# Seams of an eleven-tile feed-forward: spreading a norm's stores, a third early row tile, blocks between products

## Chip, cores and metric

The kernel runs on one core of one Trainium2 chip. The metric is device microseconds (us) of one execution; lower is better. TensorE (PE) has a granted clock of two levels, 1.2 and 2.4 GHz; the profile writes 1.00 where all of a stretch ran at 2.4 GHz.

## The reference, cut to what matters

One layer over 1024 tokens of width 1024, all in float32: a mixing stage (two recurrences), cross-attention into 256 memory tokens, a SwiGLU feed-forward of width 2816, and a final norm.

```python
h = h + (gate_a * y_a + gate_b * y_b) @ w_out
u = rmsnorm(h, norm_xa_g); m = rmsnorm(mem, norm_mem_g)
q = u @ xa_wq; k = m @ xa_wk; v = m @ xa_wv        # 4 heads of 256
h = h + softmax(q k^T / 16) v @ xa_wo
u = rmsnorm(h, norm_ffn_g)
h = h + (silu(u @ ffn_w1) * (u @ ffn_w3)) @ ffn_w2
return rmsnorm(h, norm_final_g)
```

## The kernel before

**Numbers.** Every float32 operand is split in two parts, `hi` (a copy rounded to the matmul's type) and `lo` (source minus hi); a product is three matmuls, hi·hi, hi·lo and lo·hi (`mm3`, L298). `split` (L278) writes hi on ScalarE (ACT) at L281 and lo on GpSimd (POOL) or VectorE (DVE) at L285.

**Order of work.** The mixing stage (about 0 to 1300 us) has its order written out by hand. All that follows is ordered by the framework when the kernel is compiled: each engine gets one queue, filled by priority (position in the program; a block of `high_priority` moves its instructions ahead) among what the framework's own estimate holds ready. On the chip each queue then runs strictly in that order, and an instruction whose operand is late holds all behind it. Nearly all DMAs are issued on SyncE's queue (SP), so a store that waits for its data holds the loads behind it.

**Attention** (`attention_block`, about 1300 to 1710 us). At its start the first block of `xa_wv` is loaded on ACT's queue and split, both at high priority (L1681), while the last steps of mixing (`sa`, its store to `y_d`, and two key products `pproj<-mT,wkey`) are still to run. K and V follow, block by block, then the output projection of mixing (`w_out`, tiles `pw`), the heads, and the output projection of attention (`xa_wo`, `pw` again), which runs once for each half of 512 tokens. Each projection has 4 column blocks; `load_w` loads and splits four weight tiles for each. Beside the projections `w2_sums` (L1707) makes four sums of blocks of `ffn_w2` for each of 11 rows f: load `y` (2 DMAs of 512 KB), two DVE and two POOL subtractions (L1717 to L1720), and a store of 1 MB to `wsum_d`. Seven rows go beside `w_out` and four beside the first half's `xa_wo`. `add_project` stores the new residual `h_d` after all of a half is done.

**Feed-forward, first part** (about 1710 to 2170 us). The two halves of tokens, of hidden rows and of model columns form 2x2 blocks, multiplied with 7 products in place of 8 (P1 to P7). P5 and P4 need only blocks of the second half of tokens (`S1`, `B22`), which exist before attention is through. For the first AHEAD = 2 of 11 row tiles they are made early (`early_products`, L2035), with weights loaded at high priority, and kept in SBUF (tag `kept`, 14 buffers). Then `late_blocks` (L1947) loads the first operands' rows back (`hn`), normalizes them, and in four steps k transposes them (tiles `pth`) and makes the five other blocks (B11, B21, S3, S2, S4). Then `products(f)` runs for 11 row tiles; it loads the same weights again (tag `wraw`, 10 buffers).

**Feed-forward, second part** (about 2175 to 2380 us). Seven blocks b of 11 items f each. An item is a load of an activation tile `tl` (hidden rows or their sums), a load of a weight tile `wraw`, ACT's `th` and `wh`, DVE's `tl` minus `th` (L2201), POOL's `wl` (through `operand`, L1927), and four `mm3`, which are 12 matmuls of 128x512. Loads run 8 items ahead and splits 4. When a block is done, its function (`p1`, `p6`, `p5`, `p7` or `add`) adds the four sums to the residual `hres`. A list `later` postpones some of these adds, one for each following item. When block 4 is done the first half is complete, and `add` calls `finish` for its four row tiles at once: two DVE scalings (L2139, L2143) and two stores to the output. Block 6 does this for the second half, at the very end.

Of the kernel before, what the change touches and what calls it, by code (L numbers as in the profile page):

```python
# [183 lines left out]
def tile_trunk(ctx, tc, x, mem, norm_mix_g, w_in, rw_mu, rw_w0, rw_w2, rw_a0, rw_a2, rw_g2,  # L184
# [1462 lines left out]
    def attention_block(xctx):  # L1647
# [11 lines left out]
        px = xctx.enter_context(tpool(name="xa_x", bufs=3, space=PSUM))  # L1659
        W = 256  # L1660

        def load_w(src, col, lo_eng=None, queue=nc.sync):

            s3 = src[0, :, col:col + W].rearrange("(k p) c -> p k c", p=P)
            w = []
            for k in range(0, KT, 2):
                raw = rp.tile([P, 2, W], F32, tag="wraw", name="wraw")
                queue.dma_start(out=raw, in_=s3[:, k:k + 2, :])
                hi, lo = (wp.tile([P, 2, W], F32R, tag=n, name=n) for n in ("whi", "wlo"))
# [8 lines left out]
        Vl = vp.tile([P, NMT, D], F32R, tag="Vl", name="Vl")  # L1678
        mT = [act1.tile([P, 2, 4, NM], F32R, tag=n, name="mT") for n in ("ah", "al")]
        with tc.high_priority(4000):  # L1680
            w0 = load_w(xa_wv, 0, queue=nc.scalar)  # L1681
            for n in range(2):
                for e in range(2):
                    nc.sync.dma_start(out=mT[e][:, n].bitcast(F32).rearrange("p k t -> p (k t)"), in_=md[e, n])
        for c in range(D // W):
            if 2 * c >= KEYS:
                w = load_w(xa_wk, c * W)
                for t in range(2):
                    ps = pp.tile([P, HALF], F32, tag="proj", name="pk")
                    for k in range(KT):  # L1690
                        mm3(ps[:, 0:NM], w[k][0][:, t * P:(t + 1) * P], w[k][1][:, t * P:(t + 1) * P],
                            *(m[:, k // 4, k % 4, :] for m in mT), k == 0, k == KT - 1)
                    h = Kh[:, 2 * c + t, :]
                    nc.scalar.activation(h, ps[:, 0:NM], AF.Copy)
                    nc.vector.tensor_tensor(Kl[:, 2 * c + t, :], ps[:, 0:NM], h.bitcast(F32), op=ALU.subtract)
            w = load_w(xa_wv, c * W) if c else w0
            ps = pp.tile([P, NMT, W], F32, tag="proj", name="pvv")
            for t in range(NMT):
                for k in range(KT):
                    mm3(ps[:, t, :], *(m[:, k // 4, k % 4, t * P:(t + 1) * P] for m in mT), *w[k], k == 0, k == KT - 1)  # L1700
            h = Vh[:, :, c * W:(c + 1) * W]
# [5 lines left out]
        def w2_sums(fs, places):  # L1707


            def load(f, y):  # L1710
                for r in range(2):
                    rows = slice((f + r * HF) * P, (f + r * HF + 1) * P)
                    nc.sync.dma_start(out=y[:, 2 * r:2 * r + 2, :].rearrange("p c t -> p (c t)"), in_=ffn_w2[0, rows, :])

            def sums(f, y):
                y11, y12, y21, y22 = (y[:, n, :] for n in range(4))
                nc.vector.tensor_tensor(y11, y12, y11, op=ALU.subtract)  # L1717
                nc.gpsimd.tensor_tensor(y12, y22, y12, op=ALU.subtract)
                nc.gpsimd.tensor_tensor(y22, y22, y11, op=ALU.subtract)
                nc.vector.tensor_tensor(y21, y22, y21, op=ALU.subtract)  # L1720
                nc.sync.dma_start(out=wsd[f], in_=y)

            loaded = []
            for place in places:
                if place:
                    y = place()
                    f = next(fs)
                    load(f, y)
                    loaded.append((f, y))
                    if len(loaded) < 3:  # L1730
                        yield
                        continue
                if loaded:
                    sums(*loaded.pop(0))
                yield
            for l in loaded:
                sums(*l)
                yield

        def add_project(a, w, src, halves, ss=None, beside=iter(()), every=False):  # L1740


            hs = []
            for c in range(D // W):
                ww = load_w(w, c * W)
                for i2 in range(2 * halves.start, 2 * halves.stop):
# [9 lines left out]
                    for n in range(2):  # L1756
                        o = hs[2 * i2 + n - 4 * halves.start][:, c * W:(c + 1) * W]
                        nc.vector.tensor_tensor(o, ps[:, n, :], o, op=ALU.add)  # L1758
                        if ss is not None:
                            junk = sp.tile([P, D], mybir.dt.bfloat16, tag="junk", name="junkw", bufs=1)[:, 0:W]  # L1760
                            nc.scalar.activation(junk, o, AF.Square, accum_out=ss[:, 2 * i2 + n - 4 * halves.start, c:c + 1])
                    if every or c > 1 or c == 1 and i2 % 2:
                        next(beside, None)
            return hs
# [35 lines left out]
        def in_act2(tag, n):  # L1800
# [3 lines left out]
                return pairs[tag][:, n]  # L1804
            return place

        hs = add_project(yT, w_out, x[0], range(NHALF), every=True, beside=w2_sums(
            w2f, [None, None] + [in_act2(tag, n) for tag in ("ah", "al", "ah") for n in range(2)] + [in_act2("al", 0)]))
        xaT = []
        for h in range(NHALF):  # L1810
            for i in range(4):
# [75 lines left out]
                prev = attended(oT[h], hd, next(wt))  # L1887
        for _ in prev:
            pass
        in_kv = [lambda p=p, t=t: p.tile([P, 4, HALF], F32, tag=t, name="y2")  # L1890
                 for p, t in ((kp, "Kh"), (kp, "Kl"), (vp, "Vh"), (vp, "Vl"))]

        for h in range(NHALF):
            hs = add_project(oT, xa_wo, h1d, range(h, h + 1), *((ssq, early_blocks(hs, *fa)) if h else ()),
                             **({} if h else dict(beside=w2_sums(w2f, in_kv), every=True)))
# [31 lines left out]
    def operand(t, name):  # L1927
        if isinstance(t, tuple):
            return t
        hi, lo = (wp.tile(list(t.shape), F32R, tag=n, name=n + name, bufs=7) for n in ("wh", "wl"))  # L1930
        split(hi, lo, t)
        return hi, lo

    def psum(name):
# [11 lines left out]
    def late_blocks():  # L1946
# [22 lines left out]
        for k in range(HK):  # L1969
# [47 lines left out]

    tt = nc.vector.tensor_tensor

    def weights(f):  # L2020

        return [[raw(w, k, (f + e) * P, HK, P) for e in (0, HF) for k in (0, HK)] for w in WS]

    def early_operands(A):
        T1, T4 = [], []
# [9 lines left out]
    def early_products(f, T1, T4):  # L2035

        for name, T, b in (("P5", T1, "S1"), ("P4", T4, "B22")):
            for n in range(2):
                t = kept[f, name, n] = fp.tile([P, HALF], F32, tag="kept", name=name, bufs=14)
                nc.scalar.activation(t, product(name, T[n], B[b]), AF.Copy)  # L2040

    def products(f, A):
        U2, U3, P7, T1 = [], [], [], []
# [47 lines left out]
    next(late)  # L2091
    for f in range(AHEAD):
# [23 lines left out]
    def add(h, i, c, acc, op, first):  # L2116
# [17 lines left out]
    def finish(h, i, c, order):  # L2134
        r = ss[h][:, 3, i:i + 1]
        rows = slice((4 * h + i) * P, (4 * h + i + 1) * P)
        o1, o2 = hs[h][:, 2 * i + 1 - c, :], hs[h][:, 2 * i + c, :]
        if h == 0:
# [3 lines left out]
        nc.sync.dma_start(out=out[rows, (1 - c) * HALF:(2 - c) * HALF], in_=o1)  # L2142
        ins = nc.vector.scalar_tensor_tensor(o2, o2, r, fgs[c], op0=ALU.mult, op1=ALU.mult).ins  # L2143
        if order:
            behind(ins, order)
        nc.sync.dma_start(out=out[rows, c * HALF:(c + 1) * HALF], in_=o2)

    def more(h, i, c, t):
        o = hs[h][:, 2 * i + c, :]
        tt(o, o, t, op=ALU.add)  # L2150

    later = []

    def p1(i, acc):
        nc.scalar.activation(U[i], acc, AF.Copy)
        later.append((0, i, 0, U[i]))

    def p6(i, acc):
        tt(U[i], acc, U[i], op=ALU.add)

    def p5(i, acc):
        tt(V[i], acc, U[i], op=ALU.add)
        later.append((0, i, 1, V[i]))
        later.append((1, i, 1, V[i]))

    def p7(i, acc):
        tt(U[i], acc, U[i], op=ALU.add)
        later.append((1, i, 0, U[i]))
        add(1, i, 1, acc, ALU.add, True)

    w2 = lambda r, c: lambda f: raw(ffn_w2, f + r * HF, c * HALF, 1, HALF)
# [25 lines left out]
    def split_item(b, f):  # L2197
# [10 lines left out]
    for n, (b, f) in enumerate(items):  # L2208
# [47 lines left out]
```

## Time and profile before

| what | value |
|---|---|
| median of 3 runs | 2383.24 us (2382.25 to 2384.34) |
| profiled execution | 2381.83 us |
| its span, first to last instruction | 2380.1 us |
| PE busy | 2311.5 us, 97% of the span |
| PE idle | 68.6 us |
| mean granted clock of PE | 0.990 |
| DVE, ACT, POOL busy | 64%, 48%, 52% |

A group of rows below names its view. A row of the timeline gives start, duration, engine, line, operation, out<-in, count, and in brackets the idle time of the engine before it with what ended that. A row of the windows gives a stretch, its length, busy time and count of PE, weight loads, DVE, ACT and POOL, the granted clock of PE, the busy share of the DMA engines and their rate.

### The profile page before, as it was taken

How to read it: one execution, taken by the hardware profiler on the slowest of the kernel's cores; microseconds unless marked ns; L12 is line 12 of the kernel's file. 1: busy time of each engine (PE TensorE's matmuls, PEld its weight loads, DVE VectorE, ACT ScalarE, POOL GpSimd, SP SyncE). 2: the span in 40 equal slices, each digit the busy share in tenths (PEclk: the TensorE clock that was granted, in tenths of full speed). 3: DMA queues.
4: the chain of work that ended last, by engine and by line, in shares of the span. 5: the costliest groups of instructions: out<-in, count | busy, mean ns of one | idle time of the engine just before them, and what ended most of it. 6: DMA issues, size and time to landing. Idle time of an engine off the chain costs nothing. (4 is left out here: it accounts for less than half of the span.)

```text
span 2380.1 us, 48890 instructions
## 1 busy us (share of the span) xinstructions
PE 2311.5 (97%) x19126; PEld 1913.0 (80%) x19126; DVE 1515.4 (64%) x2397; ACT 1136.1 (48%) x2271; POOL 1235.6 (52%) x1257
## 2 busy tenths in 40 slices
PE   7999999999999999999999999999989999999997
PEld 5777777778887878888887998889968888888876
DVE  5887874667777667766755545444577565566454
ACT  6545454545566646565564515442452333334432
POOL 3554545555566555675564741113465655556544
PEclk9999999999999999999999999999999999999999
DMA  5444445333334344434244893128643433348552
GB/s 176 116 126 119 124 119 166 70 95 85 103 102 121 78 130 107 114 90 115 64 150 142 272 339 128 63 70 305 201 136 100 128 100 100 111 151 319 181 173 93
DMA packets 397668, 325.97 MB, mean 137 GB/s; under 512 B 107467, under 2 KB 330813, under 8 KB 396029
## 3 DMA queue, kind: packets, MB, share of 16 engines
q1 hardware_dynamic: 395005, 317.08, 43.9%
q0 software_dynamic: 1344, 4.72, 0.5%
q8 instruction: 151, 2.47, 0.4%
q10 hardware_dynamic: 1088, 1.05, 0.1%
q14 instruction: 80, 0.66, 0.1%
HBM read 226.03 MB, written 96.21 MB: 135 GB/s over the span
## 5 line engine op out<-in xcount | busy, mean ns | idle before, releaser
L102 PE MATMUL pproj<-uh,whi 128*128 128x512 f32 x768 | 320.3, 417 | 0.9 <-DVE q L102 0.7
L102 PE MATMUL pproj<-uh,wlo 128*128 128x512 f32 x768 | 301.0, 392 | 3.2 <-POOL wlo L102 2.3
L102 PE MATMUL pproj<-ul,whi 128*128 128x512 f32 x768 | 301.4, 392 | 0.0
L285 POOL TENSOR_TENSOR wl<-wraw,wh 128x512 fp32r<-128x512 f32 x143 | 202.0, 1427 | 153.3 <-ACT wh L281 139.9
L285 POOL TENSOR_TENSOR wlo<-wraw,whi 128x512 fp32r<-128x512 f32 (+1 forms) x86 | 118.3, 1380 | 227.7 <-ACT whi L281 219.1
L281 ACT ACTIVATE whi<-wraw 128x512 fp32r<-128x512 f32 (+1 forms) x166 | 101.0, 617 | 188.4 <-DMA wraw<-in_w_out_dram 46.1
L102 POOL TENSOR_TENSOR wlo<-wraw,whi 128x512 fp32r<-128x512 f32 x96 | 128.5, 1349 | 119.3 <-ACT whi L102 106.2
L299 PE MATMUL pproj<-uh,whi 128*128 128x512 f32 (+1 forms) x432 | 179.7, 416 | 0.9 <-ACT whi L281 0.6
L301 PE MATMUL pproj<-uh,wlo 128*128 128x512 f32 (+1 forms) x432 | 170.9, 396 | 1.2 <-POOL wlo L285 1.2
L102 PEld LDWEIGHTS pproj<-uh,whi 128*128 128x128 f32 x768 | 144.4, 188 | 34.1 <-DVE q L102 2.0
L300 PE MATMUL pproj<-ul,whi 128*128 128x512 f32 (+1 forms) x432 | 170.7, 395 | 0.0
L102 PEld LDWEIGHTS pproj<-ul,whi 128*128 128x128 f32 x768 | 144.4, 188 | 32.4
L102 PEld LDWEIGHTS pproj<-uh,wlo 128*128 128x128 f32 x768 | 145.0, 189 | 28.8 <-POOL wlo L102 2.7
L300 PE MATMUL pw<-wlo,ah 128*128 128x256 f32 x512 | 146.7, 287 | 6.9 <-POOL wlo L285 4.6
L299 PE MATMUL pw<-whi,ah 128*128 128x256 f32 x512 | 146.1, 286 | 1.3 <-DVE tok L1758 1.3
L301 PE MATMUL pw<-whi,al 128*128 128x256 f32 x512 | 145.8, 285 | 0.0
L285 POOL TENSOR_TENSOR wlT<-wraw,whT 128x512 fp32r<-128x512 f32 x70 | 98.5, 1419 | 68.9 <-ACT whT L281 49.4
L299 PE MATMUL acc<-wh,th 128*128 128x512 f32 x308 | 121.5, 395 | 7.2 <-ACT wh L281 7.2
L2201 DVE TENSOR_TENSOR tl<-tl,th 128x512 fp32r<-128x512 f32 x77 | 77.1, 1028 | 79.1 <-ACT th L2200 75.2
L281 ACT ACTIVATE wh<-wraw 128x512 fp32r<-128x512 f32 x143 | 86.4, 622 | 82.5 <-PE P L300 57.3
L300 PE MATMUL acc<-wl,th 128*128 128x512 f32 x308 | 122.2, 397 | 2.0 <-POOL wl L285 2.0
L102 ACT ACT_TABLE_LOAD x90 | 115.5, 1283 | 13.5 <-DVE m L102 6.4
(456 smaller groups left out, 6551.9 us busy)
## 6 DMA issues: line engine op xcount, KB each, us to landing
wraw<-in_w_in_dram SPq DMA_DIRECT2D x148, 256.0 KB
wraw<-in_ffn_w_dram SPq DMA_DIRECT2D x137, 256.0 KB
y<-in_ffn_w_dram SPq DMA_DIRECT2D x22, 512.0 KB
wsum_d<-y SPq DMA_DIRECT2D x11, 1024.0 KB
hsum_d<-s SPq DMA_DIRECT2D x44, 256.0 KB
tl<-hsum_d SPq DMA_DIRECT2D x44, 256.0 KB
wraw<-wsum_d SPq DMA_DIRECT2D x44, 256.0 KB
hid_d<-s SPq DMA_DIRECT2D x33, 256.0 KB
```

The lines of the kernel that those rows point to most:

```text
L102: r = getattr(self.engine, op)(*a, **kw)
L281: nc.scalar.activation(hi, src, AF.Copy)
L285: e.tensor_tensor(lo, src, hi.bitcast(F32), op=ALU.subtract)
L299: nc.tensor.matmul(ps, ah, bh, start=first, stop=False)
L300: nc.tensor.matmul(ps, ah, bl, start=False, stop=False)
L301: nc.tensor.matmul(ps, al, bh, start=False, stop=last)
L2201: tt(hl, hl.bitcast(F32), hh.bitcast(F32), op=ALU.subtract)
```

## The change

It changes six places. (1) Only the first `xa_wv` loads keep the high priority; their splits go to their place in the program. (2) `w2_sums` gets a list of steps, one for each group of `w_out` (8 rows: loads in groups 2, 4, 8 and 11, sums in groups 4, 5, 6, 8, 10, 12, 13 and 14) and of the first half's `xa_wo` (3 rows, in V's buffers alone). (3) The stores of `h_d` go into `add_project`. (4) AHEAD is 3; the first two tiles load in the order that T1 needs, the third at its place after the fifth early product; `late_blocks` gives one step k after the 6th, 8th, 10th and 12th early product. (5) In the second part `lo` of the weights goes to DVE for 8 of 11 items and to POOL for 3. (6) For the first half `finish` puts two scalings and a pair of stores for each row tile on `later`, and `later` gives two entries for an item while it is longer than 11.

```diff
@@ attention_block @@
         with tc.high_priority(4000):
-            w0 = load_w(xa_wv, 0, queue=nc.scalar)
+            w0 = list(load_raw(xa_wv, 0, nc.scalar))
...
-            w = load_w(xa_wv, c * W) if c else w0
+            w = load_w(xa_wv, c * W, raws=None if c else w0)
...
-            for place in places:
-                if place:
-                    y = place()
-                    f = next(fs)
+            for loads, summed in steps:
+                for place in loads:
+                    y, f = place(), next(fs)
                     load(f, y)
                     loaded.append((f, y))
-                    if len(loaded) < 3:
-                        yield
-                        continue
-                if loaded:
+                for _ in range(summed):
                     sums(*loaded.pop(0))
                 yield
-            for l in loaded:
-                sums(*l)
-                yield
...
+                    if dst is not None and c == D // W - 1:
+                        for i in (2 * i2, 2 * i2 + 1):
+                            nc.sync.dma_start(out=dst[i * P:(i + 1) * P, :], in_=hs[i - 4 * halves.start])
...
+        loads = {2: "ah", 4: "al", 8: "ah", 11: "al"}
         hs = add_project(yT, w_out, x[0], range(NHALF), every=True, beside=w2_sums(
-            w2f, [None, None] + [in_act2(tag, n) for tag in ("ah", "al", "ah") for n in range(2)] + [in_act2("al", 0)]))
+            w2f, [([in_act2(loads[g], n) for n in range(2)] if g in loads else [], int(g in (4, 5, 6, 8, 10, 12, 13, 14)))
+                  for g in range(16)]))
...
-                             **({} if h else dict(beside=w2_sums(w2f, in_kv), every=True)))
-            for i in range(4):
-                nc.sync.dma_start(out=h2d[(4 * h + i) * P:(4 * h + i + 1) * P, :], in_=hs[i])
+                             **({} if h else dict(every=True, beside=w2_sums(
+                                 w2f, [(in_v, 0), ([], 0), ([], 1), ([], 0), (in_v[:1], 1), ([], 0), ([], 1)]))))
@@ feed-forward, first part @@
                 split(th[n][k], tl[n][k], t[n], lo_eng="dve" if n == "S3" else "pool")
-        yield
+            yield
...
+        A = [{}, {}]
+        for b in (0, 2, 3, 1):
+            for n, w in enumerate(WS):
+                A[n][b] = raw(w, b % 2 * HK, (f + b // 2 * HF) * P, HK, P)
...
-    AHEAD = 2
     with tc.high_priority(600):
-        early = [weights(f) for f in range(AHEAD)]
+        early = [weights(f, True) for f in range(2)]
         early = [early_operands(A) for A in early]
     late = late_blocks()
     next(late)
     for f in range(AHEAD):
-        early_products(f, *early[f])
-    next(late)
+        for _ in early_products(f, *early[f]):
+            n += 1
+            if n == 5:
+                early.append(early_operands(weights(2, True)))
+            if n > 5 and n % 2 == 0:
+                next(late)
@@ feed-forward, second part @@
+            if h == 0:
+                finish(h, i, c, None)
+                return
...
         if h == 0:
-            nc.vector.tensor_scalar(o1, o1, r, None, op0=ALU.mult)
-        else:
-            nc.scalar.activation(o1, o1, AF.Copy, scale=r)
+            later.extend((lambda: nc.vector.tensor_scalar(o1, o1, r, None, op0=ALU.mult), last,
+                          lambda: (store(1 - c, o1), store(c, o2))))
+            return
...
-        ops[b, f] = (hh, hl, *operand(y, "2"))
+        ops[b, f] = (hh, hl, *operand(y, "2", "pool" if f % 3 == 2 else "dve"))
...
-        if later:
-            more(*later.pop(0))
+        for _ in range(2 if len(later) > HF else 1):
+            if later:
+                later.pop(0)()
```

## Rows read from the trace of the kernel before

**Rows 1.** Part 1 of the page: busy time of each engine.
```profile
PE 2311.5 (97%) x19126; PEld 1913.0 (80%) x19126; DVE 1515.4 (64%) x2397; ACT 1136.1 (48%) x2271; POOL 1235.6 (52%) x1257
```
**Rows 2.** Windows, one for each seam (columns as told above).
```profile
1299.00:1320.00 21.00, 15.05 (x104) 14.44 (x103) 5.07 (x9) 4.08 (x7) 9.03 (x9) 0.84 0.71 239
1320.00:1360.00 40.00, 37.59 (x303) 36.36 (x302) 23.73 (x27) 24.58 (x47) 25.83 (x17) 1.00 0.92 309
1374.00:1420.00 46.00, 41.40 (x328) 40.79 (x327) 18.18 (x29) 4.95 (x8) 21.34 (x16) 0.96 0.94 350
1618.00:1650.00 32.00, 28.51 (x225) 28.02 (x225) 14.68 (x21) 7.42 (x12) 16.48 (x12) 0.89 0.82 304
1724.00:1772.00 48.00, 40.60 (x176) 31.00 (x175) 35.64 (x42) 25.22 (x43) 33.75 (x23) 0.93 0.46 147
2286.00:2300.00 14.00, 11.46 (x42) 8.55 (x41) 5.42 (x7) 5.41 (x10) 5.33 (x5) 0.88 0.51 175
2318.00:2342.00 24.00, 17.54 (x66) 13.55 (x65) 14.14 (x16) 6.78 (x15) 13.14 (x10) 0.86 0.47 161
```
**Rows 3.** Timeline around the start of attention, engines ACT, DVE, PE and SP.
```profile
1308.95 0.58 ACT L102 ACTIVATE sa<-pproj 128x512 f32<-128x512 f32 x1
1309.54 1.15 ACT L281 ACTIVATE whi<-wraw 128x512 fp32r<-128x512 f32 x2
...
1310.20 0.73 DVE L285 TENSOR_TENSOR wlo<-wraw,whi 128x512 fp32r<-128x512 f32 x1 [1.62 <-ACT whi L281]
...
1309.58 5.21 PE L102 MATMUL pproj<-mT,wkey 128*128 128x256 f32 x24 [3.07 <-ACT sa L102]
...
1313.47 0.32 SPq L102 DMA_DIRECT2D y_d<-sa  x1
```
**Rows 4.** Timeline of the output projection of mixing, engines ACT, POOL and SP.
```profile
1380.33 2.89 ACT L281 ACTIVATE whi<-wraw 128x512 fp32r<-128x512 f32 x4 [17.02 <-DMA wraw<-in_w_out_dram]
...
1382.27 2.94 POOL L285 TENSOR_TENSOR wlo<-wraw,whi 128x512 fp32r<-128x512 f32 x2
...
1354.02 1.44 SPq L1713 DMA_DIRECT2D y<-in_ffn_w_dram  x3
```
**Rows 5.** Timeline of attention's output projection, first half, engines PE and POOL.
```profile
1634.61 0.39 PE L300 MATMUL pw<-wlo,ah 128*128 128x256 f32 x1 [2.47 <-POOL wlo L285]
...
1633.30 2.94 POOL L285 TENSOR_TENSOR wlo<-wraw,whi 128x512 fp32r<-128x512 f32 x2
```
**Rows 6.** Timeline of the feed-forward's start, engines PE and SP.
```profile
1731.76 3.66 PE L1974 MATMUL pth<-ident,hn 128*128 128x128 f32 x32
...
1742.63 0.79 PE L300 MATMUL P<-lB,wh 128*128 128x512 f32 x1 [3.06 <-DVE lB L1977]
...
1726.01 52.99 SPq L1924 DMA_DIRECT2D wraw<-in_ffn_w_dram  x22
```
**Rows 7.** Groups by line of DVE and POOL (2176 to 2345), PE (2206 to 2280).
```profile
L2201 DVE TENSOR_TENSOR tl<-tl,th 128x512 fp32r<-128x512 f32 x62 | 61.1, 1011 | 65.1 <-ACT th L2200 61.2 <-PE acc L301 3.9
...
L285 POOL TENSOR_TENSOR wl<-wraw,wh 128x512 fp32r<-128x512 f32 x57 | 82.2, 1456 | 68.1 <-ACT wh L281 57.1 <-DMA wraw<-in_ffn_w_dram 8.7 <-DMA wraw<-wsum_d 2.2
...
L300 PE MATMUL acc<-wl,th 128*128 128x512 f32 x110 | 42.8, 389 | 0.0
```
**Rows 8.** Waits of SP's queue (2205 to 2345): total us, times, longest.
```profile
SPq L2176 <- POOL wl L285: 60.1, 24, 5.1
```
**Rows 9.** Timeline of the second part, engines POOL, SP and ACT.
```profile
2218.33 1.29 POOL L285 TENSOR_TENSOR wl<-wraw,wh 128x512 fp32r<-128x512 f32 x1
...
2292.67 1.27 POOL L285 TENSOR_TENSOR wl<-wraw,wh 128x512 fp32r<-128x512 f32 x1 [2.08 <-ACT wh L281]
...
2322.50 0.33 SPq L2146 DMA_DIRECT2D out_dram<-hres  x1
...
2325.45 0.38 SPq L2194 DMA_DIRECT2D tl<-hid_d  x1
...
2330.90 0.63 ACT L2200 ACTIVATE th<-tl 128x512 fp32r<-128x512 f32 x1 [12.72 <-DMA tl<-hid_d]
```

More of the change, by code (lines that the diff above doesn't have):

```diff
@@ L1660, in attention_block, with load_raw @@
         W = 256
-        def load_w(src, col, lo_eng=None, queue=nc.sync):
+        def load_raw(src, col, queue=nc.sync):
             s3 = src[0, :, col:col + W].rearrange("(k p) c -> p k c", p=P)
-            w = []
             for k in range(0, KT, 2):
@@ L1668, in load_w @@
                 queue.dma_start(out=raw, in_=s3[:, k:k + 2, :])
+                yield k, raw
+        def load_w(src, col, lo_eng=None, raws=None):
+            w = []
+            for k, raw in raws or load_raw(src, col):
                 hi, lo = (wp.tile([P, 2, W], F32R, tag=n, name=n) for n in ("whi", "wlo"))
@@ L1705, in attention_block, with w2_sums @@
             nc.sync.dma_start(out=t[:, 0:KEYS, :].bitcast(F32), in_=kd[n])
-        def w2_sums(fs, places):
+        def w2_sums(fs, steps):
             def load(f, y):
@@ L1723, in w2_sums, with add_project @@
             loaded = []
-            for place in places:
-                if place:
-                    y = place()
-                    f = next(fs)
+            for loads, summed in steps:
+                for place in loads:
+                    y, f = place(), next(fs)
                     load(f, y)
                     loaded.append((f, y))
-                    if len(loaded) < 3:
-                        yield
-                        continue
-                if loaded:
+                for _ in range(summed):
                     sums(*loaded.pop(0))
                 yield
-            for l in loaded:
-                sums(*l)
-                yield
-        def add_project(a, w, src, halves, ss=None, beside=iter(()), every=False):
+        def add_project(a, w, src, halves, ss=None, beside=iter(()), every=False, dst=None):
             hs = []
@@ L1889, in attention_block @@
             pass
-        in_kv = [lambda p=p, t=t: p.tile([P, 4, HALF], F32, tag=t, name="y2")
-                 for p, t in ((kp, "Kh"), (kp, "Kl"), (vp, "Vh"), (vp, "Vl"))]
+        in_v = [lambda t=t: vp.tile([P, 4, HALF], F32, tag=t, name="y2") for t in ("Vh", "Vl")]
         for h in range(NHALF):
-            hs = add_project(oT, xa_wo, h1d, range(h, h + 1), *((ssq, early_blocks(hs, *fa)) if h else ()),
-                             **({} if h else dict(beside=w2_sums(w2f, in_kv), every=True)))
-            for i in range(4):
-                nc.sync.dma_start(out=h2d[(4 * h + i) * P:(4 * h + i + 1) * P, :], in_=hs[i])
+            hs = add_project(oT, xa_wo, h1d, range(h, h + 1), dst=h2d, *((ssq, early_blocks(hs, *fa)) if h else ()),
+                             **({} if h else dict(every=True, beside=w2_sums(
+                                 w2f, [(in_v, 0), ([], 0), ([], 1), ([], 0), (in_v[:1], 1), ([], 0), ([], 1)]))))
             if h == 0:
@@ L1925, in raw, with operand @@
         return t
-    def operand(t, name):
-        if isinstance(t, tuple):
-            return t
+    def operand(t, name, lo_eng="pool"):
         hi, lo = (wp.tile(list(t.shape), F32R, tag=n, name=n + name, bufs=7) for n in ("wh", "wl"))
-        split(hi, lo, t)
+        split(hi, lo, t, lo_eng=lo_eng)
         return hi, lo
@@ L2018, in tile_trunk, with weights @@
     tt = nc.vector.tensor_tensor
-    def weights(f):
-        return [[raw(w, k, (f + e) * P, HK, P) for e in (0, HF) for k in (0, HK)] for w in WS]
+    AHEAD = 3
+    def weights(f, early=False):
+        if not early:
+            return [[raw(w, k, (f + e) * P, HK, P) for e in (0, HF) for k in (0, HK)] for w in WS]
+        A = [{}, {}]
+        for b in (0, 2, 3, 1):
+            for n, w in enumerate(WS):
+                A[n][b] = raw(w, b % 2 * HK, (f + b // 2 * HF) * P, HK, P)
+        return [[a[b] for b in range(4)] for a in A]
     def early_operands(A):
@@ L2040, in early_products @@
                 nc.scalar.activation(t, product(name, T[n], B[b]), AF.Copy)
+                yield
     def products(f, A):
@@ L2091, in tile_trunk @@
     next(late)
+    n = 0
     for f in range(AHEAD):
-        early_products(f, *early[f])
-    next(late)
+        for _ in early_products(f, *early[f]):
[4 more added lines that the diff above has]
+                next(late)
     for f in range(HF):
@@ L2137, in finish, with store, last @@
         o1, o2 = hs[h][:, 2 * i + 1 - c, :], hs[h][:, 2 * i + c, :]
+        def store(n, o):
+            nc.sync.dma_start(out=out[rows, n * HALF:(n + 1) * HALF], in_=o)
+        def last():
+            return nc.vector.scalar_tensor_tensor(o2, o2, r, fgs[c], op0=ALU.mult, op1=ALU.mult).ins
         if h == 0:
-            nc.vector.tensor_scalar(o1, o1, r, None, op0=ALU.mult)
-        else:
-            nc.scalar.activation(o1, o1, AF.Copy, scale=r)
-        nc.sync.dma_start(out=out[rows, (1 - c) * HALF:(2 - c) * HALF], in_=o1)
-        ins = nc.vector.scalar_tensor_tensor(o2, o2, r, fgs[c], op0=ALU.mult, op1=ALU.mult).ins
+            later.extend((lambda: nc.vector.tensor_scalar(o1, o1, r, None, op0=ALU.mult), last,
+                          lambda: (store(1 - c, o1), store(c, o2))))
+            return
+        nc.scalar.activation(o1, o1, AF.Copy, scale=r)
+        store(1 - c, o1)
+        ins = last()
         if order:
             behind(ins, order)
-        nc.sync.dma_start(out=out[rows, c * HALF:(c + 1) * HALF], in_=o2)
+        store(c, o2)
     def more(h, i, c, t):
         o = hs[h][:, 2 * i + c, :]
-        tt(o, o, t, op=ALU.add)
+        later.append(lambda: tt(o, o, t, op=ALU.add))
     later = []
@@ L2155, in p1 @@
         nc.scalar.activation(U[i], acc, AF.Copy)
-        later.append((0, i, 0, U[i]))
+        more(0, i, 0, U[i])
     def p6(i, acc):
@@ L2162, in p5 @@
         tt(V[i], acc, U[i], op=ALU.add)
-        later.append((0, i, 1, V[i]))
-        later.append((1, i, 1, V[i]))
+        more(0, i, 1, V[i])
+        more(1, i, 1, V[i])
     def p7(i, acc):
         tt(U[i], acc, U[i], op=ALU.add)
-        later.append((1, i, 0, U[i]))
+        more(1, i, 0, U[i])
         add(1, i, 1, acc, ALU.add, True)
```

## The prediction

> **What bounds the kernel now.** I read the page's busy times first, then the windows, then the timelines and waits of the stretches where the windows show a loss. PE is busy 2311.5 us of a span of 2380.1 [rows 1], and the change neither adds nor removes a matmul. So all that can be won is PE's idle time, 68.6 us, and the time for which PE ran at 1.2 GHz. The windows show where the change's places lose it [rows 2]. A stretch of length L with granted clock g has lost L - busy in idle time and at most (1 - g) x L to the lower level. In the order of the rows:
>
> A, attention's start: 5.95 idle + 0.16 x 21 = 3.4, together 9.3 us. B, K and V: 2.4. C, `w_out`: 4.6 + 1.8 = 6.4. D, `xa_wo`: 3.5 + 3.5 = 7.0. E, the feed-forward's start: 7.4 + 3.4 = 10.8. F, the second part before block 4's end: 2.5 + 1.7 = 4.2. G, just after that end: 6.5 + 3.4 = 9.8. The sum is 49.9 us. It is an upper bound, because PE was also idle in some of the time at 1.2 GHz. The tail after the last matmul is untouched.
>
> **A and B: splits at their place.** On ACT, `sa<-pproj` stands behind three of the four early `whi` and runs at 1308.95; PE's key product waits 3.07 us for it and then needs 5.21 us for its 24 matmuls [rows 3]. With the splits at ordinary priority `sa` and the key product, which come earlier in the program, go first, in time that PE now spends idle. What is late next is the last early weight: its `whi` starts at 1309.54, its `wlo` ends at 1310.20 + 0.73 = 1310.9 [rows 3]. If the loads land as before, then 30 matmuls of 256 columns remain (two k steps of the first token tile, all of the second); at 19.5 us for 160 of them before (half of B's stretch, which has 303 in 37.59 [rows 2], 0.124 each) that is 3.7 us, so this product ends at 1314.6. Before, 42 remained at 1309.58 + 5.21 = 1314.8, ending at 1320.0. The gain is 5.4 us with the clock up and 1.7 if those 30 run at the lower level, as the stretch now does; the gaps that are left before 1310.9 are nearly as long as those of C, where the clock fell, so I take 4. SP stood at the store `y_d<-sa` until 1313.47 [rows 3]; with `sa` done some 7 us earlier the loads of K's and V's weights start that much earlier too, in a stretch where the DMA engines are 0.92 busy [rows 2]. Of B's 2.4 us I take 1.5. A and B: 5.5, range 1 to 9.
>
> **C: sums beside `w_out`.** The second column block's weights landed at 1380.33, and their `wlo` started on POOL at 1382.27, with sums of `y` ahead of it [rows 4]; the DMA engines are 0.94 busy in the stretch [rows 2]. The first three sums keep their groups (4, 5, 6), the later ones move back by up to four groups, and an eighth row comes in (2 MB more to move, two more DVE and two more POOL instructions). Loads that start earlier (B) help, the moved sums help only after 1400. I take 2.5, between -3 (two more POOL instructions ahead of a `wlo`, at 2.94 us for two [rows 4]) and 6.4. The eighth row's sums fall on the transposes after `w_out`, where DVE and ACT work for PE: a cost of 1, range 0 to 3 (once more the pair of POOL instructions).
>
> **D: three rows beside `xa_wo`.** PE waits 2.47 us for a `wlo` that POOL started at 1633.30 [rows 5], again behind two subtractions of `y`. Four rows become three, with one sum for each of the column blocks 1, 2 and 3 in place of two for blocks 1 and 2, and half of the loads at the start. The wait's cause goes, the time at 1.2 GHz with it. What is late next is a `y` load into the buffer that the first sum's store must leave; SP would hold the next weights behind it. I take 5 of 7.0, range 0 to 7. Moving the `h_d` stores costs nothing: the same stores, issued while PE has other groups to run; without that cover they would cost SP's issue time, some 0.3 us each like the one in [rows 3].
>
> **E: third early tile.** PE ends the eighth early product at 1731.76, does all 32 transposes in 3.66 us, and then waits for DVE and ACT, for `lB` 3.06 us in one piece [rows 6]. After the change four more products come, 48 matmuls. At 110 x 3 matmuls of the same shape in 74 us [rows 7], 0.224 each, they take 10.8 us and lie between the steps of the transposes, the first of which may start some products earlier. In the same time stand the tile's own extra works: six DVE subtractions at 1.01 (the nearest mean, [rows 7]) = 6.1 us and four POOL splits at 1.456 [rows 7] = 5.8, both under the 10.8. DVE is now busy 35.6 of 48 us and POOL 33.8 [rows 2], so there is room. The question is the third tile's weights. Its eight loads (2.1 MB) take the place of the first of the 22 that SP issues from 1726.01 [rows 6]; at the 304 GB/s of D's stretch [rows 2] they take 6.9 us and are in by 1733, and the first operand is split by about 1735, against 1731.76 plus two steps of transposes (1.8) = 1733.6. The first half of the loads makes the first two products, so I expect a wait of 0 to 2 us. Of 10.8 I take 7, range -2 (no stall goes, and the wait comes on top) to 10.8.
>
> **F: `lo` on DVE.** An item of the second part is 4 x 3 matmuls: 110 of one kind in 74 us are 27.5 items, 2.69 us each [rows 7]. The weights' splits on POOL keep a slower pace, 25 steps from 2218.33 to 2292.67 [rows 9], 2.97 us each, so the lead is eaten up by 0.28 x 25 = 7 us and PE starves at 2290. The pace is a loop: SP waits 24 times, 60.1 us in all, for a POOL split to free a `wraw` buffer [rows 8]; the load of an activation stands behind it, ACT's `th` for a later item stands before the `wh` of the next, and that before the next split. DVE takes 0.73 [rows 3] to 1.01 us [rows 7] for such a split in place of 1.456, for 8 of 11 items: 0.32 to 0.53 us less for an item, so 2.44 to 2.65, just below 2.69. I take 3 of 4.2, range 0 to 4.2. DVE's own load: 1 + 8/11 splits and 52 adds and scalings over 77 items, 2.40 instructions for an item, at 1.01 us 2.43 us, below 2.69.
>
> The rows show that DVE's `tl` split has a mean of 1.011 us here and that a like split took 0.73 where POOL did something else [rows 7, 3]. The Trainium skill (SBUF — State Buffer, Who interferes with whom) says that a DVE instruction with two SBUF inputs contends with a GpSimd instruction that reads SBUF and that the second to start blocks until the first is done. By that rule the moved splits are exposed to it, which speaks against the change, but they also take most of POOL's instructions away: by it the 0.28 us of excess would shrink with POOL's share to about a quarter, and DVE's item to about 1.9 us; the trace can't show which effect is larger.
>
> **G: `finish` spread.** At block 4's end SP stands at eight stores, each behind a DVE scaling; the last goes at 2322.50, the next activation load at 2325.45, ACT's `th` of it after 12.72 us of idleness at 2330.90 [rows 9], and PE idles 6.5 us, then runs at 1.2 GHz [rows 2]. After the change a store pair comes every third item, behind scalings issued an item earlier; SP loses at most a DVE queue's delay at each. What is late next is F's loop. The twelve new entries of `later` are used up exactly in block 5's eleven items (two in the first), so block 5's own adds find the list empty; they cost the same DVE time as now, beside matmuls. I take 8 of 9.8, range 4 to 9.8.
>
> **Sum.** 5.5 + 2.5 - 1 + 5 + 7 + 3 + 8 = 30.0 us. The bounds add up to -3 and 47. The profiled execution has 2381.83 (its span 2380.1 and 1.7 around it), so it would have 2351.8; the median of the runs is 1.4 higher, so 2353.2.
>
> **Rivals.** (1) The third tile is late: its loads queue behind `hn` and the early blocks on SP, PE waits for them in place of `lB`, and the main loads of tile 0 come 2 MB later. For it: SP is in order and E's PE wait now is also on a chain through DVE. Against: 10.8 us of cover. E turns from 7 to -2, and with C's 2.5 also gone, 30.0 - 11.5 = 18.5: 2364.7. (2) The new steps don't do what they say: the framework issues a `y` load when its buffer and SP are free, whatever its group; three go at 1354.02 [rows 4], before `w_out` has begun though they belong to group 2. Then C and D stay as they are: 30.0 - 7.5 = 22.5, 2360.7. (3) All seams close almost fully, 45 us: 2338. (4) Slower: DVE becomes the bound of the second part. It has 2.40 instructions for an item; above 2.69 / 2.40 = 1.12 us for one it is slower than PE, and `tl`'s mean is 1.01 now. At 1.3 us an item takes 3.12, 0.43 x 77 = 33 us more, F's and G's 11 are lost as well: 30 - 44 = -14, 2397. For it: DVE's queue is in order, with splits of later items ahead of urgent ones. Against: POOL, which lengthens them, is left with a quarter of its splits.
>
> **Chances.** A measurement of this kernel can tell about 0.2%, 4.8 us. The forecast 0.46 (its own range 2345 to 2358), rival 1 0.16, rival 2 0.14, rival 3 0.10, small new waits that eat up the gain to within 0.2% 0.06, rival 4 0.08. Faster is the first four, 0.86; same 0.06; slower 0.08. The range of 2340 to 2376 leaves out half of rival 3, the same and the slower: 0.19.
>
> **What would show it.** A: `sa` ahead of all four `whi` on ACT, and SP's `y_d` store before 1306. C and D: no POOL subtraction just ahead of a `wlo` that PE waits for. E: products between the transposes, no wait for `lB` above 1 us. F: splits keep 2.69 us or better, no PE wait for `wh` in blocks 2 to 4. G: no wait of ACT for an activation load as long as 12.72 us, clock 1.00 from 2200 to PE's end. The prediction is wrong if a new wait above 5 us stands at any of these seams, or if DVE is full in the second part.

## The result, and the profile after

The changed kernel takes 2357.74 us (median; 2355.75 to 2359.64), the kernel before 2383.79 beside it: a ratio of 0.9890, 95% interval 0.9873 to 0.9908. It is faster by 26 us. The forecast was 2353.2, so the time lies 4.5 us above it, at the upper end of the forecast's own range (2345 to 2358). The profiled execution has a span of 2355.5 us against 2380.1, which is 24.6 less.

The busy times of after, which answer [rows 1]:

```profile
PE 2299.9 (98%) x19126; PEld 1906.9 (81%) x19126; DVE 1540.8 (65%) x2457; ACT 1138.8 (48%) x2275; POOL 1161.3 (49%) x1201
```

PE has the same number of instructions. It idles 55.6 us in place of 68.6, and is itself busy for 11.6 us less: with the matmuls the same, those that ran at 1.2 GHz must be fewer. The windows of after at the places of [rows 2], moved by the time gained up to there (in each row: length, then busy us and instructions of PE, PEld, DVE, ACT and POOL, granted clock, DMA share, GB/s):

```profile
1300.00:1321.00 21.00, 18.74 (x126) 17.79 (x127) 8.18 (x13) 7.17 (x12) 10.73 (x11) 0.84 0.98 333
1319.00:1359.00 40.00, 36.86 (x297) 35.65 (x295) 22.55 (x25) 21.65 (x41) 22.04 (x15) 1.00 0.82 270
1372.50:1418.50 46.00, 46.00 (x386) 46.00 (x385) 19.26 (x35) 6.32 (x10) 21.23 (x16) 1.00 0.98 369
1612.00:1644.00 32.00, 29.17 (x254) 28.77 (x253) 15.81 (x21) 7.49 (x12) 17.26 (x12) 1.00 0.76 274
1715.00:1763.00 48.00, 39.30 (x175) 31.13 (x174) 40.65 (x47) 26.75 (x48) 33.78 (x23) 0.93 0.56 175
2276.00:2290.00 14.00, 14.00 (x63) 11.58 (x63) 6.16 (x10) 4.80 (x9) 1.28 (x1) 1.00 0.55 180
2309.00:2333.00 24.00, 24.00 (x108) 19.87 (x107) 19.84 (x29) 10.98 (x23) 10.70 (x7) 1.00 0.21 78
```

Read against [rows 2], C, F and G have no loss left: PE is busy for the whole of them at a granted clock of 1.00. D keeps 2.8 us of idle time, but its clock is 1.00. B has 3.1 us of idle time, after 2.4 before. A has less idle time and the same clock of 0.84. E is where nothing was won: 8.7 us idle and 0.93, after 7.4 and 0.93 before; DVE is now busy 40.65 us of 48 there.

To see what each place gave, I take the first matmul of each stage as a marker. The timeline of PE in after (start us, duration, line, operation):

```profile
1300.04 0.63 PE L102 MATMUL pyb<-ident,yn 128*128 128x128 f32 x4 [0.33 <-DVE yn L102]
...
1356.08 0.38 PE L299 MATMUL pw<-whi,ah 128*128 128x256 f32 x1
...
1451.14 1.04 PE L321 MATMUL pt<-ident,tok 128*128 128x128 f32 x8
...
1598.06 0.29 PE L299 MATMUL pw<-whi,ah 128*128 128x256 f32 x1
...
1672.92 1.04 PE L1774 MATMUL pt<-ident,tok 128*128 128x128 f32 x8
...
1700.37 0.39 PE L299 MATMUL P<-ah,whT 128*128 128x512 f32 x1
...
2138.14 0.39 PE L299 MATMUL acc<-wh,th 128*128 128x512 f32 x1
...
2347.46 0.39 PE L301 MATMUL acc<-wh,tl 128*128 128x512 f32 x1
```

The same stage with the same code differs by some us from one profiled execution to the next. So the table takes the mean over all kernels of this study that have the old or the new code in a stage (lowest to highest, and how many); the experiments follow below.

| Stage, marker to marker | part | old code, us | new code, us | gain | predicted |
|---|---|---|---|---|---|
| last `pyb` to `w_out` | A, B | 58.95 (58.65-59.29, 5) | 55.39 (53.83-56.68, 9) | 3.6 | 5.5 |
| `w_out` to its transposes | C | 99.83 (96.40-102.65, 5) | 94.49 (93.81-95.14, 9) | 5.3 | 2.5 - 1 |
| transposes and heads | - | 146.9 | 146.9 | 0 | 0 |
| `xa_wo`, first half | D | 78.00 (77.53-78.92, 5) | 75.33 (74.43-76.50, 8) | 2.7 | 5 |
| early products to second part | E | 439.77 (438.04-440.85, 5) | 437.97 (437.74-438.40, 3) | 1.8 | 7 |
| second part | F, G | 221.64 (219.16-224.64, 4) | 210.21 (209.21-213.31, 8) | 11.4 | 3 + 8 |

The gains add up to 24.8, beside 24.6 of the two spans and 26 of the medians.

### The profile page after: what moved, and what is told of

The parts are those of the page before. It is cut to its first block, busy times and chain, and to the rows that moved or that the text cites. A ratio compares the mean times of both kernels' runs of the same rounds, so it can differ in the third digit from the quotient of the medians.

```text
span 2355.5 us, 48856 instructions
## 1 busy us (share of the span) xinstructions
PE 2299.9 (98%) x19126; PEld 1906.9 (81%) x19126; DVE 1540.8 (65%) x2457; ACT 1138.8 (48%) x2275; POOL 1161.3 (49%) x1201
## 5 line engine op out<-in xcount | busy, mean ns | idle before, releaser
L285 POOL TENSOR_TENSOR wl<-wraw,wh 128x512 fp32r<-128x512 f32 x87 | 122.1, 1410 | 195.9 <-ACT wh L281 169.1
L285 POOL TENSOR_TENSOR wlT<-wraw,whT 128x512 fp32r<-128x512 f32 x72 | 103.5, 1447 | 68.7 <-ACT whT L281 58.3
L285 DVE TENSOR_TENSOR wlo<-wraw,whi 128x512 fp32r<-128x512 f32 x80 | 72.8, 910 | 75.1 <-ACT whi L281 75.0
L301 PE MATMUL acc<-wh,tl 128*128 128x512 f32 x308 | 119.9, 389 | 0.0
```

What stands on the lines that cost most here:

```text
L285: e.tensor_tensor(lo, src, hi.bitcast(F32), op=ALU.subtract)
L301: nc.tensor.matmul(ps, al, bh, start=False, stop=last)
```

## The experiments

**One part at a time.** F alone is place (5) of the change and G alone place (6), each on the kernel before.

> The kernel before with F alone: 8 of 11 weight splits of the second part on DVE, the final norm's scalings and stores left in one piece at the end of block 4. Theory: F and G are two losses at two places. F alone takes the 2.5 us of idle PE time and the 1.7 us of the lower clock before block 4's end, so 3 to 4.5 us: a ratio near 0.9985, 2379 to 2381 us, and PE still idles some 6 us after block 4's end. Rival: the loop through the POOL splits is the one cause of both, because the lead of the splits is what would carry PE over the stores; then F alone gives 10 to 15 us, a ratio of 0.994 to 0.996, and the idle time after block 4's end goes as well.

> The kernel before with G alone: block 4's scalings and stores of the first half are spread over the later items, all weight splits of the second part stay on POOL. Theory (two losses at two places): G alone takes the 6.5 us of idle time and 3.4 us of the lower clock after block 4's end, 8 to 10 us, a ratio of 0.9958 to 0.9966, and the waits before block 4's end stay. Rival (the POOL loop, at 2.97 us for an item against PE's 2.69, is what empties the lead): with G alone the lead goes on shrinking after block 4 and PE starves there for the loop in place of the stores: G alone gives 0 to 5 us, a ratio above 0.998, and the gain of the two together, 15 us, comes only when F is there too.

F alone: 2374.46 us, ratio 0.9965 (0.9952 to 0.9979). G alone: 2374.94, ratio 0.9973 (0.9962 to 0.9984). The second part takes 211.62 us with F alone and 215.10 with G alone, where the old code needs 221.64. So F gives 10.0, G 6.5, and the two together 11.4, not 16.5: they are for the most part two cures of one loss. The size of this overlap is rough, since each of the two is a single profiled execution and the four with the old code differ by 5.5 us; the windows and waits below are the firmer sign. Neither theory had it right; the rival for F (one cause, the lead) came nearest. The windows of F alone at the old places F and G:

```profile
2286.00:2300.00 14.00, 14.00 (x64) 11.58 (x63) 5.84 (x9) 5.77 (x10) 0.53 (x1) 1.00 0.53 186
2318.00:2342.00 24.00, 22.16 (x97) 17.78 (x96) 17.33 (x29) 10.30 (x22) 8.27 (x6) 1.00 0.38 132
```

The eight stores still stand in one piece after block 4, yet PE idles 1.8 us there in place of 6.5, and the clock stays at 1.00. With splits that keep PE's pace, PE enters the stores with its items split ahead; before, the lead had been used up by 2290. G alone leaves the pace as it was, and PE goes on waiting for it a little at a time (waits of PE in the second part: total us, times, longest):

```profile
PE acc L300 <- POOL wl L285: 2.7, 3, 1.0
PE acc L299 <- ACT wh L281: 1.2, 3, 0.6
```

In after no such row is left. With the old code PE waits 6.5 to 9.2 us in the second part, with F alone 1.8. One execution with the new code, that of main_subs_behind (below), has a wait of 1.6 us for a DVE split, and its second part takes 213.31 us; so DVE's splits can be late as well.

E alone is place (4) on the kernel before, A alone place (1), and C with D places (2) and (3).

> The kernel before with E alone: a third row tile's four early products, the steps of the second half's blocks between products. Theory (DVE is full there: six subtractions more and the main tile's own ones stand ahead of lB): no gain, between -2 and +2 us, a ratio of 0.999 to 1.001, with the lower clock again somewhere between 1725 and 1775. Rival (E works as predicted and was eaten up in the full change by what C and D move into its stretch): 5 to 9 us faster, a ratio of 0.996 to 0.998.

E alone: 2380.30 us, ratio 0.9991 (0.9981 to 1.0001). Its stage takes 438.40 us, as in after. E has no gain of its own to be eaten up; the rival falls.

> The kernel before with A alone: the early loads of the first value weights stay early, their splits at their place. Theory: sa and both key products run before the value weights' splits, and SP passes the y_d store earlier; the gain is what the markers of the full change show between the end of mixing and the first transposes' start, 3 us by the start of w_out, and some of C's gain as well because w_out's loads start earlier: 3 to 6 us in all, a ratio of 0.9975 to 0.9987. Rival: the gain at K and V is only the shift of a wait, and w_out's loads, with the DMA engines 0.94 busy, take it back: 0 to 1 us, a ratio above 0.9995.

A alone: 2376.98, ratio 0.9977 (0.9968 to 0.9987). The medians differ by 5.5 us; by the markers 2.9 of them are A's own: from the last `pyb` to `w_out` it takes 56.10 us, and `w_out` then 99.76, as before. A's earlier loads gave C nothing. The rest lies in stages whose code is unaltered (the second part's 219.16 us are the least of the old code).

> The kernel before with C and D alone: the sums of y at later column groups of w_out with an eighth row, three rows beside xa_wo and the h_d stores as each row pair is done. Theory (the markers of the full change: 4.6 us less from the start of w_out to the first transposes and 3.0 us less in xa_wo's first half): most of it is C and D's own, 5 to 8 us, a ratio of 0.9966 to 0.998. Rival (C's gain came from A, whose earlier store of y_d lets w_out's loads start earlier): w_out stays within 1.5 us of before, D alone is left, 2 to 4 us, a ratio of 0.9983 to 0.9992.

C and D alone: 2375.68, ratio 0.9960 (0.9946 to 0.9973). `w_out` takes 95.14 us and `xa_wo`'s first half 74.73, as in after: both gains are C and D's own, and the rival (A) falls. Together they are 8.0 us by the markers, the top of what was expected; the ratio lies just beyond it (0.9966 was the lowest).

**Why E gave so little.** The waits of PE in after's stage E, and the windows of its worst 30 and 20 us:

```profile
PE P L299 <- ACT hB L1974: 4.0, 1, 4.0
PE P L300 <- DVE lB L1975: 2.8, 1, 2.8
PE P L299 <- ACT whT L281: 1.8, 2, 0.9
```

```profile
1720.40:1750.40 30.00, 21.30 (x100) 16.43 (x99) 28.25 (x30) 17.90 (x32) 24.88 (x17) 0.95 0.59 175
1740.40:1760.40 20.00, 13.14 (x49) 10.03 (x47) 16.52 (x18) 10.39 (x17) 18.06 (x13) 0.83 0.36 105
```

The third tile itself is late by 1.8 us only (`whT`), within the forecast's 0 to 2. But `lB`, the wait it was to cover, is still there, with `hB` beside it, because DVE is busy 28.25 of 30 us. Its timeline shows with what:

```profile
1726.31 3.46 DVE L2036 TENSOR_TENSOR wraw<-wraw 128x512 f32<-128x512 f32 x2
1729.69 0.74 DVE L1975 SCALAR_TENSOR_TENSOR lB<-pth,VC,hB 128x512 fp32r<-128x512 f32 x1
1730.35 1.28 DVE L2037 TENSOR_TENSOR wraw<-wraw 128x512 f32<-128x512 f32 x2
1731.55 0.74 DVE L1975 SCALAR_TENSOR_TENSOR lB<-pth,VC,hB 128x512 fp32r<-128x512 f32 x1
...
1742.60 1.62 DVE L2065 TENSOR_TENSOR T<-wraw 128x512 f32<-128x512 f32 x1
1744.14 0.74 DVE L1979 SCALAR_TENSOR_TENSOR fS<-pth,VC,fS 128x512 f32<-128x512 f32 x1
...
1745.82 1.76 DVE L2066 TENSOR_TENSOR wraw<-wraw 128x512 f32<-128x512 f32 x1
1747.50 1.75 DVE L2067 TENSOR_TENSOR wraw<-T,wraw 128x512 f32<-128x512 f32 x1
1749.18 1.40 DVE L1975 SCALAR_TENSOR_TENSOR lB<-pth,VC,hB 128x512 fp32r<-128x512 f32 x2
```

The third tile's subtractions (L2033 to L2037, 7.1 us) stand ahead of the second step's `lB`, those of the main loop's first tile (L2065 to L2067, 9.7 us) ahead of the third's and fourth's. ACT's `hB` of the fourth step waits behind `hS`, which waits for DVE's `fS`, and that stands behind one of these subtractions (L2065):

```profile
1744.91 0.63 ACT L281 ACTIVATE hS<-fS 128x512 fp32r<-128x512 f32 x1 [1.09 <-DVE fS L1979]
1745.45 1.25 ACT L1974 ACTIVATE hB<-pth,VC 128x512 fp32r<-128x512 f32 x2
```

Three kernels take this apart, each from the changed kernel:

```diff
# no_third_subs
+            if sub:
                 tt(a21, a21, a11, op=ALU.subtract)
# third_subs_first
-        early = [weights(f, True) for f in range(2)]
+        early = [weights(f, True) for f in range(AHEAD)]
# main_subs_behind
-            tt(T1[-1], a21, a11, op=ALU.subtract)
+            ins = tt(T1[-1], a21, a11, op=ALU.subtract).ins
+            if f == 0:
+                behind(ins, last[0])    # the S4 sum of the last step
```

> The changed kernel without the third tile's six subtractions on DVE: its loads, splits, products and copies stay, so this tile's early products are made of plain weights and the output is another. Theory (E fell because DVE is full between 1718 and 1753, where the six take 2.37 + 3.46 + 1.28 = 7.1 us ahead of lB): the steps of the second half's blocks move up by up to 7 us, the two waits of PE for hB and lB (4.0 and 2.8 us) shrink to 2 us or less together and the lower clock there goes: 5 to 9 us faster than the changed kernel, a ratio to before of 0.985 to 0.987. Rival (the third tile's weights are late, or POOL and ACT are the bound there): loads and splits are unchanged, so the seam stays as it is: 0 to 2 us, a ratio of 0.988 to 0.989.

2350.40 us, ratio 0.9863 (0.9849 to 0.9878); the stage takes 429.39 us, 8.6 less than the 437.97 of the table. The wait for `hB` is gone and one of 2.3 us for `lB` is left, at a clock of 1.00; the two were to be 2 us or less. The rest is as the theory said. With the same loads PE waits 0.6 us for the third tile's weights in place of 1.8.

> The changed kernel with the third tile's loads and subtractions together with those of the first two tiles, so that the six subtractions come before the scalings of hn, in the 10 us in which DVE waits for hn (1708.3 to 1718.5), and its splits on POOL in POOL's 10.7 us of idleness. Theory (DVE is full): nothing is left out and the full stretch gets 7.1 us shorter: 4 to 8 us faster than the changed kernel, a ratio to before of 0.985 to 0.988. Rival (SP is the bound: eight loads ahead of hn's, some 6 us by the 8 that take 4.6 to 7 us before): hn and with it every step comes 5 to 6 us later, and the time stays, 0.988 to 0.990.

2353.28, ratio 0.9873 (0.9857 to 0.9888), but the stage takes 436.84, only 1.1 less, and the rest lies in stages whose code is unaltered. Here the rival has it: DVE did the six in its idle time, but `hn`'s loads, behind eight more on SP, start 15.0 us after the first early product in place of 6.2, and PE waits 3.2 us for `hn` and 2.8 for `lB`. The theory's cure was wrong, its diagnosis not.

> The changed kernel with the main loop's first tile held back on DVE: its six subtractions (T and wraw, 9.6 us between 1735.5 and 1749.2) go behind the last step of the second half's blocks in place of ahead of the lB of the third and fourth step. Theory (DVE is full and its order decides): lB of the fourth step comes 5 to 9 us earlier, PE's wait of 4.0 and 2.8 us goes for the most part, and the six are still in time, since their first product comes four products (11 us) after the seam: 4 to 8 us faster than the changed kernel, a ratio to before of 0.985 to 0.988. Rival (the six are urgent, or POOL's splits bound the steps): PE waits for the T3 operand or for lS instead, 0 to 2 us, a ratio of 0.988 to 0.989.

2352.20, ratio 0.9865 (0.9852 to 0.9879); the stage takes 432.22, 5.7 less. Nothing is left out here, only DVE's order is another. Its windows, which answer the two of after above:

```profile
1720.00:1750.00 30.00, 28.06 (x132) 22.26 (x131) 27.13 (x32) 19.50 (x35) 22.84 (x17) 1.00 0.52 153
1740.00:1760.00 20.00, 19.30 (x84) 15.27 (x84) 17.05 (x18) 11.81 (x20) 17.55 (x13) 1.00 0.37 106
```

DVE is nearly as busy as before (27.13 of 30 us), and PE is now busy for 28.06 in place of 21.30. So what cost was not the amount of DVE's work alone but which of it came first. A last group on one chip, beside the changed kernel:

> The changed kernel unaltered, for a comparison on the same chip with the three kernels that go with it. Expected: a ratio to before of 0.988 to 0.9905. From the start of the early products to the start of the second part 437 to 439 us, a lower clock within it.

2357.31 us, ratio 0.9890 (0.9876 to 0.9905), stage E 437.74.

> main_subs_behind once more, beside the changed kernel on the same chip. Theory (DVE's order decides at this seam): 4 to 6 us faster than the changed kernel measured beside it, a ratio to before lower by 0.0016 to 0.0026, and 431 to 433 us from the early products to the second part in place of 437 to 439. Rival (the 5.5 us between the two profiled executions are the spread of executions): no difference beyond 1.5 us.

2354.16, ratio 0.9874 (0.9859 to 0.9888): 3.2 us less by the medians, 5.8 less in the stage (431.91). The stage's gain has come twice (and a third time in both_behind below, 432.34); in the whole time it is less than the 4 to 6 us expected, and the two intervals overlap.

```diff
# two_tiles_behind
-    AHEAD = 3
+    AHEAD = 2
...
+    for _ in late:
+        pass
# both_behind, in w2_sums beside xa_wo
+                if held:
+                    for n in range(2):
+                        behind(ins[n], lo_name[n])
```

> main_subs_behind with two early row tiles in place of three; the first two steps of the second half's blocks stay between the second tile's products, the other two follow them. Theory (the four products of the third tile are the cover under which DVE makes the four steps): DVE needs about 4.7 us for a step from 1718.5 on, PE has its eight products and transposes done by about 1724.5 and only 1.35 us of the first two main products to do for each step, so PE idles some 6 to 8 us and the gain over the changed kernel is lost: a ratio of 0.988 to 0.9905. Rival (DVE's order is all, the third tile gives nothing, since it brings 7.1 us of subtractions to the engine that is full): within 2 us of main_subs_behind.

2358.41, ratio 0.9894 (0.9879 to 0.9909); the stage takes 438.05. With the main loop's subtractions held as here, the third tile is worth 6 us. The place was not the expected one: PE waits 1.9 us for `hB` and 6.6 for the `T3` operand, because the held subtractions come only after the fourth step (and after a sum for which DVE waits 1.8 us). PE, without the third tile's four products, gets there first. An order of DVE that suits two tiles was not run, so what the third tile is worth against that stays open.

> main_subs_behind, and beside xa_wo's first half the first POOL and the first DVE subtraction of each sum of y go behind the last wlo of the same column block on that engine. Theory (the two waits of PE that are left in xa_wo, 0.97 us for a POOL wlo and 1.85 us for a DVE wlo, are these sums standing ahead of the splits): xa_wo's first half goes from some 75 to some 72.5 us, 2 to 3 us faster than main_subs_behind, a ratio to before of 0.985 to 0.986. Rival (the splits are late because ACT's whi waits for PE's last read of the buffer, and the later sums hold the next rows' loads and with them SP): 0 to -1 us, or slower by up to 3 us.

2351.52, ratio 0.9869 (0.9852 to 0.9885), the fastest of its group, 2.6 us below main_subs_behind and 5.8 below the changed kernel beside it; the ratio is above the 0.985 to 0.986 expected. `xa_wo`'s first half takes 72.67 us where the eight others with the new code take 74.43 to 76.50. The theory held at its place: on POOL both subtractions of `y` now follow the `wlo` pair, and on DVE one of the two `wlo` goes first.

```profile
1612.84 3.00 POOL L285 TENSOR_TENSOR wlo<-wraw,whi 128x512 fp32r<-128x512 f32 x2 [19.51 <-ACT whi L281]
1616.47 1.67 POOL L1724 TENSOR_TENSOR y<-y 128x512 f32<-128x512 f32 x1 [0.63 <-DVE y L1723]
...
1613.45 1.24 DVE L285 TENSOR_TENSOR wlo<-wraw,whi 128x512 fp32r<-128x512 f32 x1 [4.15 <-ACT whi L281]
1614.61 1.78 DVE L1723 TENSOR_TENSOR y<-y 128x512 f32<-128x512 f32 x1
```

## Why the prediction held, and which step failed

**A and B** were to give 5.5 and gave 3.6, all at A. The mechanism was right on ACT and PE: `sa` stands ahead of all four `whi`, and both key products come first. Two sizes were off. The value weights' loads land one by one until 1309.7, and PE waits for their splits four times (0.59, 0.52, 0.35 and 0.77 us). After the third of them PE runs at the lower level again (the window has a granted clock of 0.84). This is nearer the case for which the prediction had 1.7 than the one for which it had 5.4. And the `y_d` store was to come before 1306; it came at 1308.78. SP waits 4.0 us for a load of the value weights and then 3.2 for POOL's last step of `sa`, and on POOL a `wlo` of these weights still stands ahead of that step:

```profile
1306.23 1.28 POOL L285 TENSOR_TENSOR wlo<-wraw,whi 128x512 fp32r<-128x512 f32 x1 [2.05 <-ACT whi L281]
1307.47 1.28 POOL L102 TENSOR_TENSOR sa<-sa,sb 128x512 f32<-128x512 f32 x1
...
1308.78 0.32 SPq L102 DMA_DIRECT2D y_d<-sa  x1
```

So not all splits went behind `sa`, and B's 1.5 did not come.

**C** was too small at 2.5: 5.3, near its bound of 6.4 (the later sums move back by up to three groups, not four), and the eighth row cost nothing that shows (146.9 us for transposes and heads either way). **D** was too large at 5: 2.7. Three rows in place of four did away with the lower clock but not with the wait. By both_behind its cause is the one named, sums ahead of the `wlo`; the claim that "the wait's cause goes" with one sum for a column block was wrong. The first sum still stands ahead of the `wlo` on POOL, which had been idle for 19.4 us before it; that the framework put it there because it held POOL to be free is inferred. This is close to rival 2's mechanism, at this place alone.

**E is the step that failed**: 7 forecast, 1.8 measured. The loads, on which the prediction put its doubt (rival 1), cost at most the 1.8 us of the `whT` waits, within the 0 to 2 it gave them. What failed is the sentence that DVE has room because it is busy 35.6 of 48 us. The mean hid that the added subtractions go into the 30 us in which DVE makes `lB`, the very thing PE waits for, and that DVE works in order. "Both under the 10.8" of four products compared DVE's work with PE's cover, where it had to be added to DVE's own chain: four steps, 7.1 us of the third tile and 9.7 us of the main loop's first tile.

**F and G** were right as a sum, 11 against 11.4, and wrong as a division. The pace read from [rows 9] was the right cause, and it was priced only until block 4's end. But G's 6.5 us of idle time were for the larger part the price of that lost lead, as F alone shows. Rival 4 did not come. In the stretch that answers [rows 7], the groups of DVE and POOL in after are:

```profile
L2225 DVE TENSOR_TENSOR tl<-tl,th 128x512 fp32r<-128x512 f32 x62 | 46.7, 766 | 50.8 <-ACT th L2224 46.0 <-PE acc L301 4.8
L285 DVE TENSOR_TENSOR wl<-wraw,wh 128x512 fp32r<-128x512 f32 x46 | 36.1, 789 | 0.4 <-ACT wh L281 0.2
...
L285 POOL TENSOR_TENSOR wl<-wraw,wh 128x512 fp32r<-128x512 f32 x17 | 24.5, 1441 | 106.7 <-ACT wh L281 90.0 <-DMA wraw<-wsum_d 7.8 <-DMA wraw<-in_ffn_w_dram 7.0
```

DVE's `tl` fell from a mean of 1011 ns to 766 as POOL's splits went from 57 to 17. DVE was busy 112.8 of 169 us in this stretch, 1.80 us for each item of 2.69, not the 2.43 that the terms had.

That the total came out near is in part luck: C's surplus (3.8) and the second part's (0.4) made up for a part of what A and B (1.9), D (2.3) and E (5.2) fell short.

## What to carry to other kernels

Before work is moved under idle time of PE, ask what PE waits for in that idle time, and whether the new work goes to that engine, ahead of it in its queue: a mean busy share over a longer stretch does not tell. Where two losses follow each other, the first may be what makes the second so costly: a lost lead is paid later, at the next disturbance. And a place in the program is not a place in an engine's queue: here the subtractions that ran ahead of urgent work had to be tied behind it by an explicit order.

## What the runs showed of the hardware

The length of a DVE instruction depended on its operands and on POOL. In main_subs_behind the subtractions of one tile, all of one shape and with both inputs in SBUF, run once beside POOL and once without it:

```profile
1744.97 3.48 DVE L2068 TENSOR_TENSOR T<-wraw 128x512 f32<-128x512 f32 x2
1748.37 0.68 DVE L2071 TENSOR_TENSOR wraw<-wraw 128x512 f32<-128x512 f32 x1
1748.97 0.68 DVE L2072 TENSOR_TENSOR wraw<-T,wraw 128x512 f32<-128x512 f32 x1
1749.58 0.68 DVE L2071 TENSOR_TENSOR wraw<-wraw 128x512 f32<-128x512 f32 x1
1750.18 1.77 DVE L2072 TENSOR_TENSOR wraw<-T,wraw 128x512 f32<-128x512 f32 x1
...
1744.79 3.11 POOL L285 TENSOR_TENSOR lS<-fS,hS 128x512 fp32r<-128x512 f32 x2 [0.49 <-ACT hS L281]
1749.86 5.75 POOL L285 TENSOR_TENSOR wlT<-wraw,whT 128x512 fp32r<-128x512 f32 x4 [1.96 <-ACT whT L281]
```

They take 1.74 and 1.77 us beside POOL's splits and 0.68 where they began in POOL's pause (1747.90 to 1749.86). `lB`, which reads `pth` from PSUM, took 0.74 at 1729.69 and 0.70 each at 1749.18 in after, the latter beside a POOL split. The Trainium skill (SBUF — State Buffer, Who interferes with whom) says that a DVE instruction with two SBUF inputs contends with a GpSimd instruction that reads SBUF and that one with at most one such input does not, and here the trace agrees.

This is how the six added subtractions came to 7.1 us in place of 4.1 (6 x 0.68): four of them ran beside POOL's splits, and the last two, in POOL's pause from 1729.22 to 1731.83, took 1.28 together. It also fits the fall of `tl`'s mean in the second part. POOL pays too: in the kernel before, an addition of `sa` on POOL that began at 1310.35, beside the DVE split of 0.73 us in [rows 3], took 1.74 us, and the next one 1.28.
